# Small-array products of a hybrid encoder step: the planner of the order takes neighbours of one form as one piece

## The chip, the cores and the metric

The kernel runs on one core of one Trainium2 chip. The metric is the device time of one execution in microseconds. The kernel before the change took 3188.85 us (median of three runs, 3184.88 to 3190.59).

## What is computed

One layer of a streaming encoder for 2048 prompt frames and 32 sample frames, width 1024. Cut to what matters here, the token mixer has two halves that share one projection, and its outputs meet in one output projection:

```python
# A: 8 heads x 64; each 64-frame chunk sees itself and the 8 chunks before it
s = einsum('...qhd,...khd->...hqk', q, k) * 64 ** -0.5 + bias      # "s"
p = softmax(where(valid, s, -1e30))                                # "u", "sums"
o = einsum('...hqk,...khd->...qhd', p, v)                          # "po"
# B: gated linear attention, 4 heads, key 64, value 128
w = exp(where(causal, bcum_i - bcum_j, -inf))
scores = einsum('nbihd,nbjhd,nbijhd->nbhij', q, k, w)              # "g_s"
o = scores @ v + (q * exp(bcum)) @ state                           # "g_o"
state = decay * state + k_dec^T v                                  # "g_st"
y = concat(o_a, rmsnorm(o_b) * gain * silu(r)) @ w_o               # "wops"
```

Cross-attention into 256 memory tokens and a SwiGLU network of hidden width 2816 follow, with an RMSNorm before and after each sub-layer. The inputs and outputs are fp32.

## The kernel before

The program runs in stages that follow each other and overlap at their ends: the input projections (to about 578 us), the token mixer with the first three quarters of the output projection (578 to about 1220 us), the last quarter with the folding of the memory keys and values, the cross-attention, and the SwiGLU network (from about 1900 us to the end). Large products go through TensorE as three products of a high and a low part in the reduced fp32 form; the attention's values and the scores of the gated half are plain fp32, which TensorE does in two passes (two records a product in the trace).

**The mixer stage.** For each tile of 128 frames and each pair of heads of half A: scores `s` (L1051), softmax on DVE and ACT, transposes `pt` of the probabilities (L1074), and then `values` (from L1054). It makes up to five products for each of the two heads (L1058, 128 rows by 64 columns of the array, written `128*64` in the profile; head e writes partitions 64e to 64e+63 of the bank `po`), takes the reciprocals of the softmax sums on DVE (L1059), spreads these over the partitions with two more products of the same form (L1061), copies them to SBUF on ACT (L1063) and multiplies on DVE (L1064). There is one bank for `po`.

For each tile of half B and each of its two pairs of heads: 15 products a head of 64 rows by 64 columns (L1244 and L1249, `64*64`), into one PSUM bank a head, written in the code so that the two heads and the two halves of the output alternate. ACT and DVE read each bank (L1259, L1260). The two banks have the tag "gla", which has two buffers that nearly all products of half B take in turn. The state update `g_st` (L1295) has the form `128*64` too. Between these products stand those of the full form, 128 by 128: `s`, `pt`, the memory keys and values `mkps` and `mvps`, and the output projection `wops` (L1316).

**What sets the order.** Nothing of the order above is final. When all instructions are recorded, the class `Order` reads them (`_read`), gives each a duration (`_cost`), and plays the program through with a list scheduler (`_pass`): each engine takes the ready instruction of the highest priority, buffers of a tag are given in turn, and priorities come from a pass backwards. Of eight such passes the one that ends first by the planner's own figures is kept, and `queue` ties the instructions of each engine into that order. Before the change every instruction is an item of its own, and an item of TensorE costs the same whatever stands before it.

Of the kernel before, what the change touches and what calls it, by code (L numbers as in the profile page):

```python
# [18 lines left out]
P = 128  # L19
# [28 lines left out]
class Order:  # L48
# [8 lines left out]
    GATE = 5  # L57
    SLOW = 1.0
    PASSES = 7
    ROOM = (208 * 1024, 16 * 1024)  # L60

    def __init__(self, tc):
# [22 lines left out]
    def _cost(self, ins, kind, eng, outs, inps):  # L85

        n = self._free(outs[0])
        if eng == "PE":
            if any(a.tensor.name.startswith(("ident", "anti")) for a in inps):
                return (max(30.0, n * 0.86) if n < 128 else 110.0), 250.0  # L90
            if any(a.dtype == F32 for a in inps):
                if n <= 64 and list(inps[0].ap)[0][1] <= 64:
                    return 82.0, 300.0
                if n == 128 and list(outs[0].ap)[0][1] == 64:
                    return 125.0, 300.0
                if n == 512 and list(outs[0].ap)[0][1] == 32:
                    return n * 0.42, 300.0
                return 2 * max(n * 0.84, 60.0 if n < 128 else 108.0), 300.0
            t = n * 0.4385 + 6.5
            return (max(t, 111.0 if n >= 128 else 60.0) if n < 256 else t), 250.0  # L100
        if eng == "SP":
            total = 1
            for _, c in outs[0].ap:
                total *= c
            row = min(self._run(a) for a in inps[:1] + outs)
            return 540.0, total / row * (8 + 0.18 * row) / 16
        if kind == "InstMemset":
            t = 60 + n * 0.5
        elif eng == "Activation":
            if kind == "InstActivation":  # L110
                t = 172 + n * 0.9 + (190 if len(outs) > 1 else 0) + (80 if len(inps) > 1 else 0)
            else:
                t = 170 + n * 0.88 if outs[0].dtype == F32R else 165 + n * 0.83
        elif eng == "Pool":
            t = 180 + n * 2.17
        elif kind == "InstTensorReduce":
            m = self._free(inps[0])
            t = 60 + m * 1.95 if list(inps[0].ap)[-1][0] != 1 else 150 + m * 1.05
        elif kind == "InstReciprocal":
            t = 148 + n * 6.3  # L120
        elif kind == "InstTensorScalarPtr":
            t = 215 + n * 1.04 if len(inps) > 2 else 150 + n * (0.8 if self._inside(outs + inps) else 1.06)
        else:
            t = 150 + n * 1.06 + (52 if kind == "InstCustomDveAnt" and len(inps) > 2 else 0)
        return t * self.SLOW, 90.0

    @staticmethod
    def _inside(aps):
# [9 lines left out]
    def _cells(ap):  # L138
# [22 lines left out]
        p0 = ap.offset // row  # L161
        return p0, p0 + pat[0][1], bits

    def _add(self, ins, eng, cost, lane, prio, pred, use):
        self.ops.append(ins)
        self.eng.append(eng)
        self.dur.append(cost[0])
        self.lat.append(cost[1])
        self.lane.append(lane)
        self.prio.append(prio)  # L170
        self.pred.append(pred)
        self.uses.append(use)

    def _read(self, traced):
# [6 lines left out]
        for p in self.tc.info.pools:  # L181
            if p.space != DRAM:
# [3 lines left out]
                    closed[p.release_inst.name] = p.id  # L186
                for t in p.alloc_inst.bass_pool_tiles or ():
                    owner[t.name] = p.id
        stack, gone, gate, inside = {}, {}, {}, {}
        for ins in traced:  # L190
            kind = type(ins).__name__
            eng = str(ins.engine).split(".")[-1]
            if ins.name in opened:
                p, space, size, right = opened[ins.name]
                lo = max([q[2] for q in stack.values() if q[0] == space and not q[3]], default=0)
                if right:
                    lo = min([q[1] for q in stack.values() if q[0] == space and q[3]], default=self.ROOM[space == PSUM]) - size
                stack[p] = (space, lo, lo + size, right)
                before = [q for q, (s, a, b) in gone.items() if s == space and a < lo + size and lo < b]
                if before:  # L200
                    gate[p] = len(self.ops)
                    self._add(None, self.GATE, (0.0, 0.0), 0, 0, sorted({i for q in before for i in inside.get(q, ())}), [])
            elif ins.name in closed:
                space, lo, hi, _ = stack.pop(closed[ins.name])
                gone = {q: v for q, v in gone.items() if not (v[0] == space and lo <= v[1] and v[2] <= hi)}
                gone[closed[ins.name]] = (space, lo, hi)
            if kind in ("BassTilePoolBoundary", "InstLoadActFuncSet") or eng not in self.ENGINES:
                continue
            outs = [a.bass_ap for a in ins.outs if hasattr(a, "bass_ap")]
            inps = [a.bass_ap for a in ins.ins if hasattr(a, "bass_ap")]  # L210
            i = len(self.ops)
            pred, use = set(), []
            for aps, wr in ((inps, False), (outs, True)):
                for ap in aps:
                    t = ap.tensor
                    if type(t).__name__ != "Tile":
                        continue
                    k = tile_of.get(t.name)
                    if k is None:
                        k = tile_of[t.name] = len(self.tiles)  # L220
                        self.tiles.append(t)
                        log.append([])
                    if t.space == PSUM:
                        p0, p1, bits, wr_ = 0, P, 1, True
                    else:
                        p0, p1, bits = self._cells(ap)
                        wr_ = wr
                    keep = []
                    for e in log[k]:
                        j, w, q0, q1, b = e  # L230
                        if j != i and (wr_ or w) and q0 < p1 and p0 < q1 and b & bits:
                            pred.add(j)
                        if not (wr_ and j != i and p0 <= q0 and q1 <= p1 and not b & ~bits):
                            keep.append(e)
                    keep.append((i, wr_, p0, p1, bits))
                    log[k] = keep
                    if t.space != DRAM and k not in use:
                        use.append(k)
                        p = owner.get(t.name)
                        inside.setdefault(p, []).append(i)  # L240
                        if p in gate:
                            pred.add(gate[p])
            self._add(ins, self.ENGINES.index(eng), self._cost(ins, kind, eng, outs, inps), self._lane(kind, eng, outs + inps), ins.bass_priority, sorted(pred), use)
        n = len(self.ops)
        self.succ = [[] for _ in range(n)]
        for i in range(n):
# [130 lines left out]
    def queue(self):  # L377
        self._read(self.block.bb.instructions)
        n = len(self.ops)
        best = None  # L380
        prio = self.prio
        for turn in range(self.PASSES + 1):
            start, end = self._pass(prio)
            if best is None or max(end) < best[0]:
                best = (max(end), start)
            if turn == self.PASSES:
                break
            back, fin = self._pass([-(s + d) for s, d in zip(start, self.dur)], back=end)
            whole = max(fin)
            prio = [whole - b for b in fin]  # L390
        start = best[1]
        tail = {}
        for i in sorted(range(n), key=lambda i: (start[i], i)):
            e = self.eng[i]
            if e == self.GATE:
                continue
            if e in tail:
                self.tc.add_manual_dep(self.ops[i], self.ops[tail[e]].name, self.edge, reason="order of issue")
            tail[e] = i


@with_exitstack
def encoder_step(ctx, tc, ins, outs):
    nc = tc.nc
    ACT, DVE, POOL, SP = nc.scalar, nc.vector, nc.gpsimd, nc.sync
    PE = nc.tensor
# [159 lines left out]
    with ExitStack() as ph:  # L566
# [341 lines left out]
        for b in range(len(PB)):  # L908
            ops, tail = operands(b, raw)
# [25 lines left out]
    with ExitStack() as ph, ExitStack() as dn:  # L935
# [117 lines left out]
        def values(dst, v, prts, sums, rows, n, name):  # L1053

            po = po_.tile([P, 512], F32, tag="po", name=name)
            for j, kk in enumerate(rows):
                for e in range(2):
                    PE.matmul(po[e * 64 : e * 64 + 64, :n], lhsT=v[:kk, j, e * 64 : e * 64 + 64], rhs=prts[e][:kk, j, :n], start=j == 0, stop=j == len(rows) - 1)  # L1058
            DVE.reciprocal(sums[:n], sums[:n])  # L1059
            for e in range(2):  # L1060
                PE.matmul(po[e * 64 : e * 64 + 64, P : P + n], lhsT=sums[:n, e : e + 1].broadcast_to([n, 64]), rhs=ident[:n, :n], start=True, stop=True)  # L1061
            rec = up.tile([P, P], F32, tag="rec", name=name + "_rec", bufs=2)
# [426 lines left out]
        order, fin_at = [0] * 7 + [1], []  # L1489
# [27 lines left out]
        for i in range(total + LAG):  # L1517
# [11 lines left out]
            gen, n = dense[b]  # L1529
            k = -(-n // max(1, size - off - DEND[b])) if off >= DSTART[b] else 0  # L1530
            if off == DSTART[b] - 1 and b:
                k = 1
# [673 lines left out]
```

## Time and profile before

| | before |
|---|---|
| median of three runs | 3188.85 us |
| the profiled execution | 3188.78 us |
| its span | 3187.0 us |
| TensorE busy, share of the span | 3069.1 us, 96% |
| VectorE, ScalarE, GpSimd busy | 72%, 49%, 24% |
| granted TensorE clock, mean | 0.984 |

The span runs from the first instruction to the last. A busy engine in this profile is one that has an instruction under way; ends of TensorE's products are modelled, and products overlap, so the distance from one start to the next says more than the length of one.

### The profile page before, as it was taken

What the parts mean: (1) busy time and instruction counts of PE and PEld (TensorE: products, weight loads), DVE (VectorE), ACT (ScalarE), POOL (GpSimd) and SP (SyncE); (2) the same over time, 40 slices, a digit from 0 to 9 for tenths busy, and PEclk for the clock granted to TensorE, in tenths of its full rate; (3) what the DMA queues carried; (4) which work ended last, traced back from release to release, by engine and by line L of the source; (5) the groups of instructions that cost most, each with busy time, mean ns of one, the idle gap of its engine ahead of it and who ended that gap; (6) DMA issues with size and microseconds to landing.
All of it is one profiled execution on the core that took longest, in us unless ns stands there. A gap on an engine that the chain in (4) does not pass through costs nothing.

```text
span 3187.0 us, 56680 instructions
## 1 busy us (share of the span) xinstructions
PE 3069.1 (96%) x21363; PEld 2835.7 (89%) x21363; DVE 2292.6 (72%) x4226; ACT 1558.1 (49%) x3338; POOL 768.1 (24%) x908
## 2 busy tenths in 40 slices
PE   7899999899999999999999999999899999999998
PEld 7889999687877778889898798999889999999997
DVE  7987976566666767635547778888987778887776
ACT  5646655565665655533324434444533334633333
POOL 0201000346556554322212011111041111121111
PEclk8999999899999999999999999999999999999999
DMA  5568373875665757523225465444464445344444
GB/s 152 182 169 292 104 219 123 263 221 169 204 227 176 213 180 227 156 85 106 82 78 173 147 204 182 165 169 148 130 204 146 146 146 172 112 163 146 146 146 164
DMA packets 419011, 528.64 MB, mean 166 GB/s; under 512 B 47056, under 2 KB 324793, under 8 KB 418705
## 3 DMA queue, kind: packets, MB, share of 16 engines
q1 hardware_dynamic: 418737, 525.02, 51.6%
q8 instruction: 168, 2.75, 0.4%
q14 instruction: 106, 0.87, 0.1%
HBM read 384.05 MB, written 141.98 MB: 165 GB/s over the span
## 4 chain that ended last, share of the span: by engine, by line
PE 87%; DVE 6%; DMA 2%; ACT 2%; issue 1%; POOL 1%; SPq 0%; DVEq 0%; POOLq 0%; ACTq 0%
PE pu_X L473 8%; PE pg_X L473 7%; PE pdX L473 7%; PE wops L1316 6%; PE mo L473 5%; PE ms L473 5%; PE pu_Y L473 4%; PE pg_Y L473 4%; PE pdY L473 3%; PE po L1058 3%; PE s L1051 2%; PE pt L1074 2%; PE pu_Z L473 2%; PE g_s L1249 2%; PE pg_Z L473 2%; PE pdZ L473 2%
## 5 line engine op out<-in xcount | busy, mean ns | idle before, releaser
L433 POOL TENSOR_TENSOR u<-g,u 128x692 fp32r<-128x692 f32 (+1 forms) x111 | 195.5, 1766 | 1132.9 <-ACT u L432 967.0
L473 PE MATMUL pg_X<-mf,wg_s 128*128 128x346 f32 (+1 forms) x1584 | 285.7, 328 | 12.6 <-ACT wg_s L432 3.0
L473 PE MATMUL pu_X<-mf,wu_s 128*128 128x346 f32 (+1 forms) x1584 | 280.6, 324 | 3.2 <-ACT wu_s L432 2.3
L473 PEld LDWEIGHTS pg_X<-mf,wg_s 128*128 128x128 f32 x1584 | 261.0, 192 | 20.7 <-ACT wg_s L432 3.7
L473 PEld LDWEIGHTS pu_X<-mf,wu_s 128*128 128x128 f32 x1584 | 258.2, 190 | 8.1 <-issue 3.4
L473 PE MATMUL pdX<-u,wd 128*128 128x346 f32 (+1 forms) x1440 | 239.8, 325 | 8.8 <-issue 8.1
L473 PEld LDWEIGHTS pdX<-u,wd 128*128 128x128 f32 x1440 | 233.7, 192 | 10.3 <-issue 9.3
L1316 PE MATMUL wops<-om,wo_s 128*128 128x512 f32 (+1 forms) x960 | 222.3, 365 | 2.5 <-ACT om L437 1.3
L432 ACT CAST wg_s<-wg_r 128x512 fp32r<-128x512 f32 x231 | 136.5, 620 | 179.9 <-DVE wg_r L520 86.4
L432 ACT CAST u<-g 128x692 fp32r<-128x692 f32 (+1 forms) x111 | 84.5, 773 | 234.9 <-PE pdX L473 172.8
L473 PE MATMUL ms<-gT,hm 128*128 128x512 f32 x768 | 190.2, 401 | 1.7 <-POOL hm L438 1.5
L473 PE MATMUL mo<-pT,hT 128*128 128x256 f32 x1536 | 191.5, 283 | 0.1
L473 PEld LDWEIGHTS mo<-pT,hT 128*128 128x128 f32 x1536 | 185.7, 188 | 1.7 <-DVE my L1650 0.3
L433 DVE TENSOR_TENSOR wu_s<-wu_r,wu_s 128x512 fp32r<-128x512 f32 x231 | 163.8, 736 | 28.7 <-ACT wu_s L432 28.4
L433 DVE TENSOR_TENSOR wg_s<-wg_r,wg_s 128x512 fp32r<-128x512 f32 x231 | 157.3, 705 | 37.2 <-ACT wg_s L432 37.0
L432 ACT CAST wu_s<-wu_r 128x512 fp32r<-128x512 f32 x231 | 136.0, 619 | 83.0 <-DVE wu_r L520 41.1
L473 PEld LDWEIGHTS ms<-gT,hm 128*128 128x128 f32 x768 | 142.3, 189 | 34.8 <-POOL hm L438 1.9
L1316 PEld LDWEIGHTS wops<-om,wo_s 128*128 128x128 f32 x960 | 151.9, 190 | 23.4 <-issue 3.1
L473 PE MATMUL pg_Y<-mf,wg_s 128*128 128x346 f32 (+1 forms) x792 | 141.8, 325 | 5.6 <-ACT wg_s L432 4.8
L473 PE MATMUL pu_Y<-mf,wu_s 128*128 128x346 f32 (+1 forms) x792 | 138.2, 322 | 0.5 <-ACT pu_c L562 0.5
L473 PEld LDWEIGHTS pg_Y<-mf,wg_s 128*128 128x128 f32 x792 | 128.2, 189 | 9.9 <-ACT wg_s L432 6.2
L523 DVE TENSOR_TENSOR acc<-acc,pdX 128x346 f32<-128x346 f32 (+1 forms) x192 | 96.2, 514 | 56.1 <-PE pdX L473 55.9
(506 smaller groups left out, 7257.1 us busy)
## 6 DMA issues: line engine op xcount, KB each, us to landing
wd<-wdd SPq DMA_DIRECT2D x140, 512.0 KB, 4.8
wdd<-wd SPq DMA_DIRECT2D x70, 512.0 KB, 3.0
wg_r<-in_w_ffn_gate_dram SPq DMA_DIRECT2D x66, 512.0 KB, 4.5
wu_r<-in_w_ffn_up_dram SPq DMA_DIRECT2D x66, 512.0 KB, 4.7
q<-qd SPq DMA_DIRECT2D x32, 512.0 KB, 4.5
wo_r<-in_w_o_dram SPq DMA_DIRECT2D x64, 256.0 KB, 3.5
wd_r<-in_w_ffn_down_dram SPq DMA_DIRECT2D x26, 512.0 KB, 4.4
nb<-nbd SPq DMA_DIRECT2D x16, 640.0 KB, 6.7
```

The costliest lines, as they stand in the source:

```text
L432: ACT.copy(hi, src)
L433: (lo_eng or DVE).tensor_tensor(out=lo, in0=src, in1=hi.bitcast(F32), op=ALU.subtract)
L473: PE.matmul(ps, lhsT=a, rhs=b, start=first and i == 0, stop=last and i == len(seq) - 1, skip_group_check=skip)
L523: eng.tensor_tensor(out=out, in0=a, in1=b, op=ALU.add)
L1051: PE.matmul(ps_out, lhsT=q[:, 2 * i + e, q0 : q0 + nq], rhs=ks[:, e, k0 : k0 + ncol], start=i == 0, stop=i == 1)
L1058: PE.matmul(po[e * 64 : e * 64 + 64, :n], lhsT=v[:kk, j, e * 64 : e * 64 + 64], rhs=prts[e][:kk, j, :n], start=j == 0, stop=j == len(rows) ...
L1074: PE.transpose(ptp[:kk, j, :n], pr[:n, c0 : c0 + kk], ident[:n, :n])
L1249: PE.matmul(sps[bk, li, :], lhsT=lh, rhs=rh, start=True, stop=True)
L1316: PE.matmul(ps, lhsT=a, rhs=b, start=i == 0, stop=i == len(seq) - 1)
```

## The change

`Order._form` names the array form of a product on TensorE that uses at most half of the rows or columns, and nothing for all others. Where two products of one such form follow each other in the recorded program, with no instruction of any engine between them, the second joins the item of the first (`_join`): durations are added, what either waits for the item waits for, and the item is put in order as one. An item of a small form costs 280 ns more (`TURN`), and two of the durations of small products are lowered. In `values` the reciprocals are recorded ahead of the products, so that they no longer stand between the products of L1058 and L1061.

```diff
@@ -57,6 +57,7 @@
     GATE = 5
     SLOW = 1.0
     PASSES = 7
+    TURN = 280.0
     ROOM = (208 * 1024, 16 * 1024)
 
     def __init__(self, tc):
@@ -90,9 +91,9 @@
                 return (max(30.0, n * 0.86) if n < 128 else 110.0), 250.0
             if any(a.dtype == F32 for a in inps):
                 if n <= 64 and list(inps[0].ap)[0][1] <= 64:
-                    return 82.0, 300.0
-                if n == 128 and list(outs[0].ap)[0][1] == 64:
-                    return 125.0, 300.0
+                    return 60.0, 300.0
+                if n <= 128 and list(outs[0].ap)[0][1] == 64:
+                    return 110.0, 300.0
                 if n == 512 and list(outs[0].ap)[0][1] == 32:
                     return n * 0.42, 300.0
                 return 2 * max(n * 0.84, 60.0 if n < 128 else 108.0), 300.0
@@ -125,6 +126,14 @@
         return t * self.SLOW, 90.0
 
     @staticmethod
+    def _form(eng, outs, inps):
+
+        if eng != "PE":
+            return None
+        form = tuple(next(w for w in (32, 64, P) if list(a.ap)[0][1] <= w) for a in (inps[0], outs[0]))
+        return None if form == (P, P) else form
+
+    @staticmethod
     def _inside(aps):
         return all(type(a.tensor).__name__ == "Tile" and a.tensor.space == SBUF for a in aps)
 
@@ -161,8 +170,16 @@
         p0 = ap.offset // row
         return p0, p0 + pat[0][1], bits
 
+    def _join(self, ins, cost, prio, pred, use):
+
+        self.ops[-1].append(ins)
+        self.dur[-1] += cost[0]
+        self.prio[-1] = min(self.prio[-1], prio)
+        self.pred[-1] = sorted(pred.union(self.pred[-1]))
+        self.uses[-1] += [k for k in use if k not in self.uses[-1]]
+
     def _add(self, ins, eng, cost, lane, prio, pred, use):
-        self.ops.append(ins)
+        self.ops.append([ins])
         self.eng.append(eng)
         self.dur.append(cost[0])
         self.lat.append(cost[1])
@@ -186,7 +203,7 @@
                     closed[p.release_inst.name] = p.id
                 for t in p.alloc_inst.bass_pool_tiles or ():
                     owner[t.name] = p.id
-        stack, gone, gate, inside = {}, {}, {}, {}
+        stack, gone, gate, inside, form = {}, {}, {}, {}, None
         for ins in traced:
             kind = type(ins).__name__
             eng = str(ins.engine).split(".")[-1]
@@ -199,6 +216,7 @@
                 before = [q for q, (s, a, b) in gone.items() if s == space and a < lo + size and lo < b]
                 if before:
                     gate[p] = len(self.ops)
+                    form = None
                     self._add(None, self.GATE, (0.0, 0.0), 0, 0, sorted({i for q in before for i in inside.get(q, ())}), [])
             elif ins.name in closed:
                 space, lo, hi, _ = stack.pop(closed[ins.name])
@@ -208,7 +226,9 @@
                 continue
             outs = [a.bass_ap for a in ins.outs if hasattr(a, "bass_ap")]
             inps = [a.bass_ap for a in ins.ins if hasattr(a, "bass_ap")]
-            i = len(self.ops)
+            was, form = form, self._form(eng, outs, inps)
+            joined = form is not None and form == was
+            i = len(self.ops) - joined
             pred, use = set(), []
             for aps, wr in ((inps, False), (outs, True)):
                 for ap in aps:
@@ -240,7 +260,13 @@
                         inside.setdefault(p, []).append(i)
                         if p in gate:
                             pred.add(gate[p])
-            self._add(ins, self.ENGINES.index(eng), self._cost(ins, kind, eng, outs, inps), self._lane(kind, eng, outs + inps), ins.bass_priority, sorted(pred), use)
+            cost = self._cost(ins, kind, eng, outs, inps)
+            if joined:
+                self._join(ins, cost, ins.bass_priority, pred, use)
+                continue
+            if form is not None:
+                cost = cost[0] + self.TURN, cost[1]
+            self._add(ins, self.ENGINES.index(eng), cost, self._lane(kind, eng, outs + inps), ins.bass_priority, sorted(pred), use)
         n = len(self.ops)
         self.succ = [[] for _ in range(n)]
         for i in range(n):
@@ -394,9 +420,10 @@
             e = self.eng[i]
             if e == self.GATE:
                 continue
-            if e in tail:
-                self.tc.add_manual_dep(self.ops[i], self.ops[tail[e]].name, self.edge, reason="order of issue")
-            tail[e] = i
+            for ins in self.ops[i]:
+                if e in tail:
+                    self.tc.add_manual_dep(ins, tail[e].name, self.edge, reason="order of issue")
+                tail[e] = ins
 
 
 @with_exitstack
@@ -1053,10 +1080,10 @@
         def values(dst, v, prts, sums, rows, n, name):
 
             po = po_.tile([P, 512], F32, tag="po", name=name)
+            DVE.reciprocal(sums[:n], sums[:n])
             for j, kk in enumerate(rows):
                 for e in range(2):
                     PE.matmul(po[e * 64 : e * 64 + 64, :n], lhsT=v[:kk, j, e * 64 : e * 64 + 64], rhs=prts[e][:kk, j, :n], start=j == 0, stop=j == len(rows) - 1)
-            DVE.reciprocal(sums[:n], sums[:n])
             for e in range(2):
                 PE.matmul(po[e * 64 : e * 64 + 64, P : P + n], lhsT=sums[:n, e : e + 1].broadcast_to([n, 64]), rhs=ident[:n, :n], start=True, stop=True)
             rec = up.tile([P, P], F32, tag="rec", name=name + "_rec", bufs=2)
```

**What stands otherwise in the order.** The first place is TensorE in the middle of the mixer stage, at tile 12 of half B. `g12_s1` to `g12_s3` are the scores of its heads 1 to 3, `po10_3` the values of frame tile 10 and head pair 3, `s` and `pt` scores and transposes of half A. Before:

```order
L1249 MATMUL g12_s1_12730<-g12_W0_12428 64x64 x5
L1074 MATMUL pt10_7_0_12622<-ident_61,u10_7_sb_12491 128x128 x3
L1074 MATMUL pt10_7_3_12627<-ident_61,u10_7_sb_12491 128x128 x2
L1249 MATMUL g12_s1_12730<-g12_kq_12147 64x64 x2
L1058 MATMUL po10_3_12638<-prt10_6_12579,v10_3_12265 64x128
L1244 MATMUL g12_s2_12844<-g12_W1_12601 64x64
L1249 MATMUL g12_s2_12844<-g12_W1_12601 64x64 x3
L1051 MATMUL s12_1_0_12708<-ks12_0_12549,q12_0_12547 128x320 x2
L1249 MATMUL g12_s2_12844<-g12_W1_12601 64x64 x3
L1051 MATMUL s12_1_1_12711<-ks12_0_12549,q12_0_12547 128x320 x2
L1249 MATMUL g12_s2_12844<-g12_W1_12601 64x64
L1058 MATMUL po10_3_12638<-prt10_7_12621,v10_3_12265 64x128
```

After, at the second pair of heads of the same tile, where the last two rows go on by turns to 30 products (line numbers are those of the changed file, some 27 higher):

```order
L1101 MATMUL pt11_6_3_12688<-ident_61,u11_6_sb_12565 128x128 x2
L1343 MATMUL wops2_0_0_13253<-om2_4_13148,wo2_0_4_s_13250 128x512 x2
L1101 MATMUL pt11_7_0_12720<-ident_61,u11_7_sb_12616 128x128 x3
L1078 MATMUL s13_0_0_12832<-ks12_0_12549,q12_0_12547 128x320 x2
L1271 MATMUL g12_s2_12844<-g12_W1_12601 64x64
L1271 MATMUL g12_s3_12845<-g12_W1_12601 64x64
L1276 MATMUL g12_s2_12844<-g12_W1_12601 64x64
L1276 MATMUL g12_s3_12845<-g12_W1_12601 64x64
```

Before, the scores of one head were cut into short runs between products of other forms, and its neighbour's came later; after, both heads of a pair stand in one run and alternate.

The second place is TensorE earlier in the stage, between the two pairs of heads of tile 2 in the order after (`mkps4` is a memory key product, `s3_6_0` and `s3_7_0` scores of half A). Of all 16 prompt tiles this is the one with the least other work between its two pairs, by the widths of the products:

```order
L1276 MATMUL g2_s1_7379<-g2_kq_6831 64x64
L1101 MATMUL pt2_6_0_8080<-ident_61,u2_6_sb_7974 128x128
L1078 MATMUL s3_6_0_8062<-ks2_3_7869,q2_3_7867 128x512 x2
L1343 MATMUL mkps4_7177<-mm_0_6534,wmk4_0_s_7169 128x256 x6
L1343 MATMUL mkps4_7177<-mm_1_6546,wmk4_0_s_7169 128x256 x6
L1343 MATMUL mkps4_7177<-mm_2_6558,wmk4_4_s_7174 128x256 x6
L1343 MATMUL mkps4_7177<-mm_3_6570,wmk4_4_s_7174 128x256 x6
L1078 MATMUL s3_7_0_8094<-ks2_3_7869,q2_3_7867 128x512 x2
L1078 MATMUL s4_0_0_8127<-ks4_0_8053,q4_0_8051 128x320
L1271 MATMUL g2_s2_7433<-g2_W1_7220 64x64
```

Before, the four heads of this tile stood as runs of 15, 15, 15, 12 and 3, with 10 and 14 products of `mkps` between the first three; after, they are two runs of 30, with 30 products of other kinds between them.

Counted over the whole program on TensorE, in runs of products of one form: of `64*64` there are 99 runs before and 32 after (960 products), of `128*64` 178 before and 81 after (768 products). Before, 68 of the 99 and 106 of the 178 runs have an odd number of products; after, none has.

## The prediction

> **What bounds the kernel now.** The page first. These are the 40 slices (each 80 us of the span of 3187), busy tenths, granted clock and the shares of the chain of waits:
>
> ```profile
> PE   7899999899999999999999999999899999999998
> DVE  7987976566666767635547778888987778887776
> PEclk8999999899999999999999999999999999999999
> PE 87%; DVE 6%; DMA 2%; ACT 2%; issue 1%; POOL 1%; SPq 0%; DVEq 0%; POOLq 0%; ACTq 0%
> ```
>
> TensorE (PE) is busy nearly everywhere at a nearly full clock, and 87% of the chain is PE. Where the change acts is told by the windows, one for each stage; the columns are the length, then busy us and instructions of PE, PEld, DVE, ACT and POOL, the granted clock, the DMA share and GB/s:
>
> ```profile
> 0.00:578.00 578.00, 536.00 (x3555) 517.90 (x3556) 443.24 (x677) 325.71 (x610) 40.93 (x46) 0.97 0.57 177
> 578.00:1220.00 642.00, 634.09 (x5952) 502.95 (x5952) 416.57 (x1167) 403.30 (x1161) 352.05 (x630) 0.99 0.66 207
> 1220.00:1500.00 280.00, 267.00 (x1689) 238.30 (x1688) 150.11 (x253) 123.33 (x252) 88.19 (x55) 0.98 0.45 142
> ```
>
> In the mixer stage, 578 to 1220 us, PE is busy for 634 of 642 us. The next engine, DVE, has 417. So in this stage the time is PE's work plus 8 us. The waits of PE there, longest total first (total us, times, longest), confirm it:
>
> ```profile
> PE pt L1074 <- ACT u_sb L1038: 2.7, 4, 0.8
> PE mvps L1316 <- DVE mvf L1411: 1.5, 1, 1.5
> ```
>
> What PE saves here shortens the stage, as long as no other engine takes over. The affected products are the scores of half B (`g_s`) and the values (`po`). Their own windows over the same stage:
>
> ```profile
> 578.00:1220.00 642.00, 80.39 (x1920) 66.81 (x1920) 39.65 (x64) 12.87 (x64) 0.99 0.66 207
> 578.00:1220.00 642.00, 121.37 (x1376) 82.66 (x1376) 18.36 (x64) 17.13 (x64) 0.99 0.66 207
> ```
>
> The first line is `g_s`: 80 us of PE. The second is `po`: 121 us. Together that is about a third of the stage.
>
> **What a run of small products costs.** From the timeline of PE (start us, length, line, out<-in, records; a product is two records). I read distances from start to start, since the lengths overlap. First `g_s`:
>
> ```profile
> 862.00 0.32 PE L1249 MATMUL g_s<-g_kq 64*64 64x64 f32 x2
> 862.25 0.44 PE L1074 MATMUL pt<-ident,u_sb 128*128 128x128 f32 x2
> ...
> 787.93 0.27 PE L1244 MATMUL g_s<-g_W 64*64 64x64 f32 x1
> ...
> 788.80 0.28 PE L1249 MATMUL g_s<-g_kq 64*64 64x64 f32 x3
> 789.01 0.77 PE L1074 MATMUL pt<-ident,u_sb 128*128 128x128 f32 x5
> ```
>
> One product alone takes 862.25 − 862.00 = 0.25 us. The run that starts at 787.93 is one head's 15 products (30 records up to 789.01) and takes 1.08 us. Products of one head run in pairs, one on each half of the columns, so 15 products are 8 pairs: a pair costs (1.08 − 0.25)/7 = 0.119 us, and a run another 0.13 us. Once in this trace two heads happen to stand by turns in the order:
>
> ```profile
> 783.52 1.61 PE L1316 MATMUL wops<-om,wo_s 128*128 128x512 f32 x6
> 785.05 0.27 PE L1244 MATMUL g_s<-g_W 64*64 64x64 f32 x2
> ...
> 785.88 0.33 PE L1249 MATMUL g_s<-g_kq 64*64 64x64 f32 x7
> 786.13 1.20 PE L1058 MATMUL po<-prt,v 128*64 128x128 f32 x17
> ```
>
> These 60 records, 30 products, take 786.13 − 785.05 = 1.08 us, as long as 15 of one head: all four quarters of the array work at once. The order of the changed kernel makes every run like this one. Then `po`:
>
> ```profile
> 862.88 0.43 PE L1058 MATMUL po<-prt,v 128*64 128x128 f32 x2
> 863.24 0.68 PE L1249 MATMUL g_s<-g_W 64*64 64x64 f32 x16
> ...
> 817.68 1.31 PE L1058 MATMUL po<-prt,v 128*64 128x128 f32 x20
> 818.83 0.39 PE L1061 MATMUL po<-ident,sums 128*64 128x128 f32 x4
> 819.14 0.85 PE L1051 MATMUL s<-ks,q 128*128 128x320 f32 x4
> ```
>
> One product alone takes 0.36 us, twelve in a row 819.14 − 817.68 = 1.46 us: a pair costs (1.46 − 0.36)/5 = 0.22 us, a run another 0.14 us. A run also delays what stands ahead of it:
>
> ```profile
> 815.22 2.10 PE L1316 MATMUL wops<-om,wo_s 128*128 128x512 f32 x8
> 817.16 0.60 PE L1303 MATMUL g_tt<-ident,g_ob 128*128 128x128 f32 x4
> ```
>
> Eight `wops` ahead of a full-form product take 1.94 us, 0.24 each; the six at 783.52, ahead of `g_s`, take 1.53 instead of 1.46. I take 0.09 us, an estimate between these 0.07 and the 0.14 that a run costs besides its pairs.
>
> **The sum.** The runs and products are counted in the two orders (front part).
> - `g_s` before: 960 products in 99 runs, 68 of odd length, so 514 pairs: 514 × 0.119 + 99 × 0.13 = 74 us (the window says 80, with the modelled ends). After: 32 × 1.08 = 34.6 us. Saved: 39.
> - `po` and the state update before: 768 products in 178 runs, 106 odd, so 437 pairs: 437 × 0.22 + 178 × 0.14 = 121 us. After: 384 × 0.22 + 81 × 0.14 = 96 us. Saved: 25.
> - Entries: (99 − 32) + (178 − 81) = 164 fewer, × 0.09 = 15 us; where one small run follows another directly the exit was counted already, 37 times before and 8 after, so less 29 × 0.09 = 3. Saved: 12.
>
> That is **76 us of PE work** less. The reciprocals only move: 64 of them on DVE, ahead of products that wait for the exponentials and transposes anyway, while DVE is 65% busy; cost 0. If that cover were gone, each could hold up one run for its own length; the group is small:
>
> ```profile
> L1059 DVE RECIPROCAL sums<-sums x64: 145/160/168, 582.7 to 1213.0; 128x2 f32<-128x2 f32 x64
> ```
>
> At most 64 × 0.16 = 10 us then, and I take 0. The 280 ns on other small forms (gate transposes, the sample's products) change only the planner's belief; PE does the same products there. What a differently balanced order does to the other stages is not shown by any row. I bound it by what PE idles in the neighbouring ones, 42 and 13 us, as a shift of a tenth of that either way, 6 us, and take 0.
>
> **What is late next.** The same loads must come in a stage 12% shorter. On the whole that is 0.66 × 642/566 = 0.75 of the DMA engines. But two stretches of 40 us are near full:
>
> ```profile
> 580.00:620.00 40.00, 37.83 (x352) 28.35 (x352) 21.00 (x84) 27.14 (x99) 15.23 (x37) 0.92 0.94 310
> 860.00:900.00 40.00, 40.00 (x361) 32.04 (x360) 27.79 (x82) 28.66 (x72) 25.99 (x32) 1.00 0.91 307
> ```
>
> If these two do not shrink, 80/642 of the gain is lost, 9.5 us. I count that as lost. It leaves 76 − 9.5 = 66 us, 2.1%: 3188.8 (the profiled execution, span 3187.0 plus 1.8 around it, and equal to the median of 3188.85) − 66.5 = **3122 us**. Its own range is 3108 (76 saved, and 5 more elsewhere) to 3136.
>
> **The rivals.**
> - *Whole pieces wait.* A piece starts only when the last of its inputs is there: both heads' transposes for `po`, both banks for `g_s`. The planner also believes a `g_s` piece lasts 30 × 60 + 280 = 2080 ns, where the trace says 1.08 us plus the entry, so PE runs some 0.9 us ahead of plan at each of 32 pieces, 29 us in all, and may find what follows not ready. If all of these 29 us come back as waits, the time is 3122 + 29 = 3151. For it: before, the planner took 768 × 125 ns = 96 us for the `128*64` products that cost 121, so PE ran behind its plan and found its inputs ready (98.8% busy); that margin goes. Against it: DVE would be 417/566 = 74% busy and ACT 71%, so most inputs are ready early.
> - *The banks become the bound, and the kernel slower.* The rows of what reads the two banks:
>
> ```profile
> L1259 ACT COPY at<-g_s x64: 189/206/210, 593.4 to 1200.0; 64x64 f32<-64x64 f32 x64
> L1260 DVE TENSOR_TENSOR g_ms<-g_s,gmask x64: 591/620/626, 593.6 to 1212.1; 128x448 f32<-128x448 f32 x64
> ...
> L1223 ACT ACTIVATE g_W<-g_e 128x512 f32<-128x512 f32 (+1 forms) x93 | 44.6, 490 | 41.0 <-PE g_e L1222 40.6
> ```
>
>  A run of both heads fills both "gla" banks at once, and they are free after 0.21 + 2 × 0.62 = 1.45 us. If PE had nothing else to do after each of the 32 runs, it would wait 46 us. If the exponents `g_e`, which take the same two banks, were pushed behind their reader too, 93 × 0.49 = 46 us would be added. That is 92, which is 16 more than is saved: 3205. It decides from the point where the work between two runs of a tile is shorter than 1.45 us. The order speaks against it: in the tile with the least, 24 `mkps` and six others stand there. A `mkps` is 256 wide, half of a `wops` of 0.24, so this is over 24 × 0.12 = 2.9 us.
>  The Trainium skill, TensorEngine Tiling (Array Packing), section Performance Considerations, warns of just this: tiling makes TensorE faster but not the emptying of PSUM, which can become the bottleneck after a fourfold speedup. By that rule the time would end near 3205 instead of 3122; the trace so far shows DVE with time to spare, and no run here shows the tiled runs at this density yet.
> - *Nothing comes of it.* If the time lost between small runs reappears before the next product that waits for a DMA or for ACT, the stage stays at 642 us: 3189. Against it: PE waits 8 us in the whole stage.
>
> **How the numbers follow.** Forecast 0.68; whole pieces wait 0.22; banks, slower, 0.05; nothing 0.05. The range from 3102 to 3153 takes in the first two: below, the full 76 us with 6 us elsewhere (3107) and most of what an entry of 0.14 instead of 0.09 would add, (164 − 29) × 0.05 = 7 us; above, the waits with 2 us more. It leaves out the last two. A measurement of this kernel tells about 0.2% (6 us) from no change: faster by more 0.90, within 0.05, slower 0.05.
>
> **What would show it.** In the changed profile the `g_s` window should fall from 80 to about 40 us of PE, and each run of 60 records should last 1.08 us; `po` should fall from 121 to about 96. The mixer stage should be some 570 to 580 us long with PE over 96% busy. If `g_s` and `po` fall but PE's waits for ACT, DVE or DMA in the stage rise from 8 us to over 30, the first rival is right; if the waits name L1260, the second. The forecast is wrong at its root if a run of 60 records takes 1.8 us rather than 1.08.

## The result and the profile after

The changed kernel takes **3110.5 us** (median of four runs, 3108.0 to 3112.8) against 3189.7 us of the kernel before: a ratio of 0.9753, with a 95% interval from 0.9736 to 0.977. That is 79 us less; 3122 us was predicted. Its profiled execution took 3112.8 us, its span is 3111.0.

The slices, the clock and the chain of the page, as shown of before:

```profile
PE   7999999899999999999999999999999999999997
DVE  7986976476777776544457778889887779887776
PEclk9999999899999999999999999999999999999999
PE 84%; DVE 6%; DMA 3%; ACT 2%; POOL 2%; issue 2%; SPq 1%; DVEq 0%; ACTq 0%; POOLq 0%
```

PE still bounds the kernel, with a little less of the chain: 84 instead of 87%, and DMA, POOL, the issue and SPq have one point more each. To see where the 76 us between the two profiles went, I cut both at the first product of the key fold (`gps`), which ends the mixer stage. It starts at:

```profile
L473 PE MATMUL gps<-kt,wqt_s x192: 277/282/388, 1241.7 to 1310.0; 128*128 128x256 f32 x192
```

```profile
L500 PE MATMUL gps<-kt,wqt_s x192: 276/281/387, 1176.4 to 1243.7; 128*128 128x256 f32 x192
```

The first row is of before, the second of after: 65.3 us are saved up to there, and the other 10.7 us behind it. The windows on both sides of the cut, first before:

```profile
578.00:1242.00 664.00, 653.37 (x6107) 520.40 (x6107) 435.56 (x1196) 414.54 (x1183) 360.26 (x636) 0.99 0.67 210
1242.00:3187.00 1945.00, 1879.72 (x11705) 1797.41 (x11703) 1413.78 (x2354) 817.82 (x1545) 366.96 (x228) 0.98 0.45 147
```

and after:

```profile
578.00:1176.00 598.00, 578.54 (x6105) 481.50 (x6106) 432.19 (x1194) 411.39 (x1186) 365.12 (x638) 0.98 0.74 232
1176.00:3111.00 1935.00, 1873.08 (x11709) 1796.62 (x11708) 1413.94 (x2356) 818.12 (x1545) 372.02 (x229) 0.98 0.45 149
```

In the mixer stage PE does practically the same number of instructions (6105 and 6107) in 74.8 us less of busy time (653.4 to 578.5), and idles 19.5 us instead of 10.6. DVE, ACT and POOL do the same work in a shorter stage. The two groups that the change aims at, over the mixer stage of after, `g_s` first and then `po`:

```profile
578.00:1176.00 598.00, 37.40 (x1920) 32.74 (x1920) 39.73 (x64) 10.36 (x64) 0.98 0.74 232
578.00:1176.00 598.00, 89.60 (x1376) 74.21 (x1376) 18.20 (x64) 16.79 (x64) 0.98 0.74 232
```

`g_s` fell from 80.4 to 37.4 us of PE, `po` from 121.4 to 89.6, 75 us together. These windows count modelled lengths, which reach into the next product, so they don't tell what the products ahead of a small run gained. Counting every record of PE in the stage from its start to the next start, without PE's idle time, does: the scores fall from 73.5 to 35.2 us, the values with the state update from 119.2 to 94.5, and all other products by 11.6 (`pt` 6.8, `s` 2.4, `wops` 2.3). How single runs look now, from the timeline of PE after:

```profile
783.62 1.31 PE L1086 MATMUL po<-prt,v 128*64 128x128 f32 x20
784.76 0.39 PE L1088 MATMUL po<-ident,sums 128*64 128x128 f32 x4
785.08 0.44 PE L1299 MATMUL g_t<-ident,g_W 128*128 128x128 f32 x2
...
801.40 0.27 PE L1271 MATMUL g_s<-g_W 64*64 64x64 f32 x2
801.42 0.27 PE L1276 MATMUL g_s<-g_W 64*64 64x64 f32 x2
...
802.21 0.33 PE L1276 MATMUL g_s<-g_kq 64*64 64x64 f32 x7
802.48 0.55 PE L1101 MATMUL pt<-ident,u_sb 128*128 128x128 f32 x3
```

Twelve `po` products take 785.08 − 783.62 = 1.46 us, thirty `g_s` products of two heads 802.48 − 801.40 = 1.08 us, both just as read from the trace of before. Of the 32 runs of `g_s` 30 last 1.08 to 1.11 us, the other two 1.40 and 1.58. The waits of PE in the stage, longest total first:

```profile
PE mvps L1343 <- DVE mvf L1438: 4.0, 4, 2.2
PE s L1078 <- DMA ks<-kad: 2.5, 2, 2.2
PE s L1078 <- DVE u_mn L1062: 2.1, 5, 1.0
PE g_z L1229 <- DVE g_ms L1287: 1.9, 3, 0.8
PE mkps L1343 <- ACT mm L459: 1.6, 1, 1.6
PE s L1078 <- DMA x0r<-in_x_t_dram: 1.3, 1, 1.3
```

They are many and short, and no one engine stands behind them. The reader of the score banks (`g_ms`, L1287) holds up PE for only 2.1 us, 1.9 at `g_z` and 0.2 at `g_s`.

### The profile page after: what moved, and what is told of

Same layout as the page of the kernel before. It is cut to its first block, busy times and chain, and to the rows that moved or that the text cites. A ratio compares the mean times of both kernels' runs of the same rounds, so it can differ in the third digit from the quotient of the medians.

```text
span 3111.0 us, 56693 instructions
## 1 busy us (share of the span) xinstructions
PE 2986.9 (96%) x21363; PEld 2795.7 (90%) x21363; DVE 2288.7 (74%) x4226; ACT 1554.2 (50%) x3338; POOL 778.4 (25%) x908
## 4 chain that ended last, share of the span: by engine, by line
PE 84%; DVE 6%; DMA 3%; ACT 2%; POOL 2%; issue 2%; SPq 1%; DVEq 0%; ACTq 0%; POOLq 0%
PE pu_X L500 8%; PE pg_X L500 8%; PE pdX L500 7%; PE mo L500 6%; PE ms L500 6%; PE wops L1343 5%; PE pu_Y L500 4%; PE pg_Y L500 4%; PE pdY L500 3%; PE pu_Z L500 2%; PE s L1078 2%; PE pg_Z L500 2%; PE pdZ L500 2%; PE po L1086 2%; PE pdn L500 1%
## 5 line engine op out<-in xcount | busy, mean ns | idle before, releaser
L1343 PEld LDWEIGHTS wops<-om,wo_s 128*128 128x128 f32 x960 | 151.1, 188 | 23.5 <-POOL om L465 3.4
```

The source lines that it names most:

```text
L1343: PE.matmul(ps, lhsT=a, rhs=b, start=i == 0, stop=i == len(seq) - 1)
```

## The experiments

All times are medians, to be set against 3110.5 us of the changed kernel and about 3189 us of before; "cut" is the start of the first `gps` in the profile, as above. The runs of each form were counted in the built orders.

**1. The heads one after the other inside a piece.** What is tested: how much of the gain on the scores comes from four quarters of the array at work at once, and what PE's time is now worth.

```diff
                     for h, rs, sps in hs:
                         PE.matmul(sps[0:64, 7, :], lhsT=W[rs, 1, 0:64], rhs=W[rs, 1, 64:128], start=True, stop=True)
-                    for li in range(7):
-                        for bk in (slice(0, 64), slice(64, 128)):
-                            for h, rs, sps in hs:
+                        for li in range(7):
+                            for bk in (slice(0, 64), slice(64, 128)):
```

> The changed kernel, with the 15 products of one head recorded before the 15 of the other, so that a piece of 30 holds the heads one after the other. Runs of each form in the order are the same 32 and 81. Theory (half of the gain on the scores comes from four quarters of the array at once): each run of 60 records lasts 1.83 us instead of 1.08, 32 x 0.75 = 24 us more, 3110.5 + 24 = 3134.5. Rival (only the number of changes of form counts): 3110.5, within 4 us.

It took 3119.4 us, ratio 0.9779 to before (0.9764 to 0.9794): 9 us more, not 24. The windows of its mixer stage, all instructions first, then `g_s` alone:

```profile
578.00:1185.00 607.00, 595.31 (x6105) 502.05 (x6105) 431.83 (x1196) 415.16 (x1184) 365.64 (x635) 0.99 0.72 229
578.00:1185.00 607.00, 60.87 (x1920) 56.48 (x1920) 39.76 (x64) 12.72 (x64) 0.99 0.72 229
```

and one of its runs on the timeline:

```profile
800.56 0.27 PE L1271 MATMUL g_s<-g_W 64*64 64x64 f32 x1
...
802.39 0.55 PE L1101 MATMUL pt<-ident,u_sb 128*128 128x128 f32 x3
```

The mechanism is as expected: a run takes 802.39 − 800.56 = 1.83 us and the scores 60.9 us of PE, 23.5 more than in the changed kernel. But the stage is only about 9 us longer, and PE's idle time in it falls from 19.5 to 607 − 595.3 = 11.7 us. Most of what the extra work costs is made up by fewer waits and by slower stretches in the profile of the changed kernel: from 600 to 640 us the granted clock is 0.91 there, and 1.00 here. No shift of the plan is in this comparison: the planner sees the same pieces, and in the two traces PE goes through the same tiles in the same order. So the alternation of the heads frees 23.5 us of PE, and brings little more than a third of that.

**2 and 3. One form alone.** What is tested: whether the two terms of the sum stand by themselves.

For the scores, and with `(P, 64)` in the same place for the values:

```diff
-        return None if form == (P, P) else form
+        return form if form == (64, 64) else None
```

> The changed kernel, with pieces and the price of a turn for the 64*64 form alone; the 128*64 products stand in 181 runs with 433 pairs (before 178 and 437). Theory (the terms add): the scores' 39 us and 67 entries at 0.09 us = 6 are saved, 3189.7 - 45 = 3145, 3140 to 3150. Rival (the gain is one of the plan as a whole, or of either form with the other): 3125 or less, or 3165 or more.

> The changed kernel, with pieces and the price of a turn for the 128*64 form alone; the 64*64 products stand in 84 runs with 509 pairs (before 99 and 514), heads nearly always one after the other. Theory (the terms add): 53 pairs x 0.22 + 98 runs x (0.14 + 0.09) = 34 us, and 15 runs of the scores at 0.22 = 3 us, 3189.7 - 37 = 3153, 3147 to 3159. Rival (the values were waiting for their inputs anyway): 3175 or more.

The scores alone: 3145.7 us (0.9858, 0.9843 to 0.9874), 44 us less than before, as the sum gave (45). The values alone: 3145.5 us (0.9862, 0.9846 to 0.9879), also 44 us less, where the sum gave 37. The 7 us more are not explained by the counts. In this kernel's order the first `s` stands ahead of the products `g_z` and `g_e` that come before it in the kernel before, and starts at 569.5 us instead of 579.0; that the 7 us come from there is not shown, since the profiled execution took 3137.6 us, 8 less than the median. The two gains add up to 88 us, while the kernel with both (experiment 5) gained 74. The 14 us that are missing agree with experiment 1, but every one of these kernels has its own plan, and experiment 8 shows that new plans alone can differ by nearly as much.

**4. The reciprocals back between the products.** What is tested: the share of the second part of the change. `DVE.reciprocal` stands behind the loop over the rows again.

> The changed kernel, with the reciprocals recorded between the products of the values again, which parts each piece of 12 into 10 and 2. The order has 117 runs of 128*64 instead of 81, with the same 384 pairs. Theory (each run costs 0.14 + 0.09 us besides its pairs): 36 x 0.23 = 8 us more, 3119. Rival (freer pieces fit the order better and give it back): 3110.5 or less.

It took 3117.8 us (0.9771, 0.9756 to 0.9785), close to the 3119 of the theory, but its interval overlaps that of the changed kernel, and its runs spread from 3111 to 3120. Its profiled execution took 3111.4 us, 6 less than the median, and there the first `gps` starts at 1176.7 us, where it starts at 1176.4 in the changed kernel. But the work of the theory is in it: `po` takes 97.8 us of PE instead of 89.6, PE is busy in the stage for 5.9 us more, and its idle time there is 14.6 us instead of 19.5. So 36 more runs do cost PE 6 to 8 us; how much of that reaches the kernel's time stays open, between nothing in the profile and 7 us in the median.

**5. No pieces of 32 rows or columns.** What is tested: where the 10.7 us behind the mixer stage come from. `_form` returns a form only for 64 by 64 and 128 by 64.

> The changed kernel, with pieces and the price of a turn for the forms 64*64 and 128*64 alone, not for those with 32 rows or columns (gate transposes, the sample's products). Theory (the sample's projections gained 5 us by standing in pairs and the rest behind the mixer stage, 6 us, is the shift of a new plan): 3115, 3112 to 3121. Rival (none of the gain behind the mixer comes from these forms): 3110.5.

It took 3115.8 us (0.9772, 0.9757 to 0.9786). The number is that of the theory, though its interval overlaps that of the changed kernel; the reason is another. The windows on both sides of its cut:

```profile
576.00:1169.00 593.00, 574.53 (x6093) 476.93 (x6092) 433.17 (x1194) 408.76 (x1179) 360.36 (x633) 0.99 0.74 233
1169.00:3115.00 1946.00, 1881.96 (x11720) 1799.97 (x11718) 1416.30 (x2356) 820.45 (x1549) 373.16 (x231) 0.98 0.45 148
```

Behind the cut it takes 1946 us, as the kernel before: all of the gain there is gone, not just half. The mixer stage instead ends 7 us earlier than in the changed kernel.

**6. The sample's products alone.** So the counterpart: pieces and the price for the form 128 by 32 of plain fp32 only, which are the products of the one sample tile.

```diff
-        if eng != "PE":
+        if eng != "PE" or any(a.dtype != F32 for a in inps) or len(outs[0].ap) and list(outs[0].ap)[0][1] <= 32 and any(a.tensor.name.startswith("ident") for a in inps):
             return None
...
-        return None if form == (P, P) else form
+        return form if form == (P, 32) else None
```

The condition on `ident` keeps transposes of 32 rows or columns out.

> The changed kernel, with pieces and the price of a turn for the form 128*32 of plain fp32 alone, which are the sample's products; reciprocals and durations as in the changed kernel. 96 and 181 runs of the two larger small forms, as before the change. Theory (the 10.7 us behind the mixer stage come from the sample's products): 3189.7 - 10.7 = 3179. Middle (only what stands in pairs is saved): 3184. Rival (they come from a shift of the plan): 3186 to 3190.

It took 3182.4 us, ratio 0.9984 (0.9975 to 0.9993): some 5 us less than the 3187.3 us of the kernel before beside it, which as a saving is about the middle case. Its windows:

```profile
578.00:1247.00 669.00, 658.40 (x6097) 520.23 (x6097) 426.83 (x1196) 414.17 (x1182) 356.51 (x631) 0.99 0.66 208
1247.00:3178.00 1931.00, 1869.62 (x11713) 1793.26 (x11711) 1413.18 (x2354) 819.32 (x1547) 373.48 (x231) 0.99 0.45 149
```

Behind the cut it takes 1931 us, 14 less than before; its mixer stage became 6 us longer and took part of that back. How the gain arises shows on PE's timeline at the sample's query projection, before:

```profile
1767.91 1.04 PE L1824 MATMUL sq_a<-sqw,s_hq 128*32 128x512 f32 x2
1768.89 1.38 PE L473 MATMUL pu_Z<-mf,wu_s 128*128 128x348 f32 x7
1770.20 1.05 PE L1824 MATMUL sq_a<-sqw,s_hq 128*32 128x512 f32 x2
1771.17 0.42 PE L473 MATMUL pu_Z<-mf,wu_s 128*128 128x348 f32 x1
```

and after:

```profile
1704.72 1.06 PE L1851 MATMUL sq_a<-sqw,s_hq 128*32 128x512 f32 x8
1705.72 1.85 PE L500 MATMUL pg_X<-mf,wg_s 128*128 128x348 f32 x10
```

One product of 32 columns takes 1768.89 − 1767.91 = 0.98 us; four of them, on the four quarters of the columns, take 1705.72 − 1704.72 = 1.00 us. PE's time in the two sample projections, `sq_a` and then `so_a`, before:

```profile
1242.00:3187.00 1945.00, 8.21 (x32) 1.24 (x32) 0.69 (x1) 0.59 (x1) 0.98 0.45 147
1242.00:3187.00 1945.00, 8.42 (x32) 1.15 (x32) 0.69 (x1) 0.59 (x1) 0.98 0.45 147
```

and after:

```profile
1176.00:3111.00 1935.00, 5.09 (x32) 0.85 (x32) 0.69 (x1) 0.59 (x1) 0.98 0.45 149
1176.00:3111.00 1935.00, 7.17 (x32) 1.11 (x32) 0.69 (x1) 0.59 (x1) 0.98 0.45 149
```

That is 16.6 against 12.3 us, 4.4 us saved directly. That the rest of the 10.7 hangs on pieces of the same form is shown by experiments 5 and 6, and by all kernels together: from the first `gps` to the end, the eight with pieces of this form take 1930.5 to 1936.5 us, the five without them 1939.7 to 1945.8 (means 1934.1 and 1943.5). Through what (idle time behind the cut fell by some 3 us too) was not followed further.

**7. Price and durations.** What is tested: whether the planner's figures do anything by themselves. Three kernels: the changed one with `TURN = 0.0`; the one before with the lowered durations alone; the changed one with figures from the trace (`TURN = 200.0`, 33 ns in place of 60).

> The changed kernel with the price of a turn at 0; pieces stay. The order has 32 and 82 runs of the two forms, as with the price. Theory (the pieces do it, the price does nothing): 3110.5, within 6 us. Rival (the price makes the plan keep time with TensorE): 3120 or more, with more waits of PE in the mixer stage.

> The kernel before with the two lowered durations of small products alone: no pieces, no price of a turn, reciprocals where they were. 93 and 182 runs of the two forms. Theory (durations alone do nothing but shift the plan): 3189.7 less 1 us for the counts, within 6 us, and this is the size of such shifts. Rival (better durations are a part of the gain): 3180 or less.

> The changed kernel, with the planner's figures set to what the trace shows: 33 ns for a 64*64 product in a piece and 200 ns for a turn, so that a piece of 30 counts 1190 ns (the trace: 1.08 us and the entry) and not 2080. Theory (PE ran ahead of a plan that gave it too much time, and its waits in the mixer stage, 15 us with the edges, come in part from that): 5 us less, 3105. Rival (the waits are those of loads and of the stage's edges): 3110.5, within 3 us.

Without the price: 3115.4 us (0.977, 0.9756 to 0.9784), with the first `gps` at 1177.3 us as good as in place. The durations alone: 3188.1 us, ratio 0.9999 (0.9989 to 1.0008), nothing. The figures of the trace: 3108.9 us (0.975, 0.9734 to 0.9766), not to be told from the changed kernel. The pieces do the work; the figures shift the plan by a few microseconds.

**8. Pieces for plain fp32 only, with both sets of figures.** What is tested: whether leaving out the products that lose nothing by a change of form makes a better plan. `_form` has the condition of experiment 6, and keeps all three forms.

> The changed kernel, with pieces and the price of a turn for plain fp32 products alone: not for the transposes of 32 rows or columns and not for products of the reduced form, which the trace shows at 121 ns before, in and behind such a run. The sample's projections still stand in longer runs. Theory (pieces without a price that TensorE does not ask for keep the mixer stage as short as without the 32s, 1169 us to the first key fold, and the 1935 us behind it as in the changed kernel): 3104 + 2 = 3106. Rival (the stages differ by the shift of a new plan alone): 3110 to 3116.

> As e9_fp32_only, and the planner's figures as in e8_calibrated (33 ns a product in a 64*64 piece, 200 ns a turn). Theory (both shifts add): 3104, 3100 to 3108. Rival (each is the shift of a new plan): within 4 us of 3110.

The first took **3105.7 us** (0.9742, 0.9728 to 0.9755), as its theory had it, with the cut at 1166.1 us; the second 3117.4 us (0.9775, 0.9761 to 0.9788), with the cut at 1182.7 us, outside both of its cases, though its figures are nearer to the trace. The first is the lowest of all medians, but its interval overlaps that of the changed kernel. And over the seven kernels with the same or nearly the same pieces in the mixer stage (the changed one, experiments 4, 5, 7 twice, 8 twice) the cut lies anywhere from 1166 to 1183 us. The same figures of the trace go with 1168.7 us (experiment 7) and with 1182.7. The theory falls: what separates these kernels is the shift of a new plan, up to 17 us in this stage by single profiles and 12 us in the medians (3105.7 to 3117.8), and not how near the figures are.

## Why the prediction was right

**PE bounds the mixer stage, and its saved time is the gain.** Right. PE's busy time there fell by 74.8 us, where 76 were summed.

**What a run costs.** Right to the hundredth: 1.08 us for 30 products by turns, 1.46 for twelve values, and 1.83 where the heads stand in sequence (experiment 1). The terms (39 for the scores, 25 for the values, 12 for the entries) are borne out one by one in PE's time from start to start: 38.3, 24.7 and 11.6 us. In the kernel's time the scores alone brought what the sum gives (experiment 2: 44 measured, 45 with their entries); the values alone brought 7 us more, which the counts do not explain.

**What is late next.** The size was right, the place only in part, so that the size came out is in part luck. The 9.5 us were to be lost in two stretches near the limit of the DMA engines. PE's idle time in the stage rose by 8.8 us. But at 860 to 900 us nothing is lost, PE is busy for 39.9 of 40 us, and at the start of the stage and near 1000 us more is lost than was foreseen. The stretch from 600 to 640 us, before and after:

```profile
600.00:640.00 40.00, 38.56 (x414) 29.82 (x410) 27.30 (x92) 26.23 (x94) 17.06 (x40) 1.00 0.80 256
```

```profile
600.00:640.00 40.00, 35.41 (x370) 29.02 (x369) 27.66 (x96) 27.70 (x97) 15.78 (x37) 0.91 0.93 298
```

PE loses 3 us to waits there, and the granted clock is 0.91 in place of 1.00, with the DMA share at 0.93. That it is the loads that hold it up was not tried by itself; the waits shown above name loads, DVE and ACT side by side.

**The other stages, taken as 0 with 6 us either way.** This is the term that was mis-sized, and it is most of the 12 us between forecast and result. The prediction said that for the small forms outside the two "PE does the same products there". It does, but the sample's projections are small products of neighbouring column quarters too, and in longer runs they overlap. That and what follows from it gave 10.7 us in the two profiles; experiments 5 and 6 and the comparison of all kernels place it with pieces of that form, and 4.4 us of it are seen directly in the two projections.

**The rivals.** *Whole pieces wait* did not come: idle time rose by 8.8 and not by 29 us. Its supposed cause, a plan that gives PE too much time for a `g_s` piece, was tested in experiments 7 and 8, and correcting the figure gained nothing that can be measured: with the same corrected figures PE idles 14 us in the stage in one kernel and 25 in the other. *The banks become the bound* did not come either. The Trainium skill, TensorEngine Tiling (Array Packing), section Performance Considerations, warns that emptying PSUM may become the bottleneck once tiling has sped up the products; this trace does not show it at this speed: `g_ms` holds PE up for 2.1 us in all, and in the order work of other kinds stands between the two runs of a tile. *Nothing comes of it* is excluded by the interval. What did show is that PE time is no longer worth its full length in the stage, as the 23.5 us of experiment 1 that cost 9 tell; the 88 against 74 us of experiments 2, 3 and 5 fit that but are not clear of the shifts of new plans. Which wait takes the rest was not found.

## What to carry to other kernels

Where a scheduler orders single instructions, look in the trace at what a lone small product costs against a row of them: here 0.25 us against 1.08 for thirty, and the changed order has 164 runs fewer. Keep products that lie on different quarters of the array next to each other, and look for all places where a form occurs: the pieces of the sample's products, of which the two projections have just 32, went with a seventh of the gain. Once PE's waits in a stage have grown (here from 10.6 to 19.5 us), discount what more is saved there, and take shifts of some 10 us from any new plan as scatter, not as a result.

## What the runs showed of the hardware

- Two heads' 64 by 64 products by turns take the time of one head's: 60 records in 1.08 us, as long as 30 of one head, against 1.83 us for the 60 with the heads in sequence.
- Going into a small form of plain fp32 and out of it cost about 0.09 us on either side. In the mixer stage of before, medians from start to start: a record of `wops` takes 0.233 us ahead of a product of the full form and 0.326 ahead of `g_s`, `po` or `g_st`, and one of `pt` 0.109 and 0.202; the last record of `po`, as wide as one of `pt`, takes 0.203 when the full form follows. Products of the reduced fp32 form with 32 columns were not held up. In this piece of the timeline of before the second row is of that form:

```profile
559.84 4.07 PE L473 MATMUL wvb_X<-wvb_s,mi 128*128 128x256 f32 x33
563.74 2.98 PE L473 MATMUL wvb_T<-wvb_s,tail 128*32 128x256 f32 x24
```

 The 33 records of the full form take 563.74 − 559.84 = 3.90 us, 0.118 each, with the change at their end; the 24 of 32 columns last 2.98 us with the modelled end of the last, 0.12 each.
